# A trunk of two decoder layers: 28 of the 44 gate/value tile pairs of the up-projections as seven quarter products, with weights summed by accumulating DMAs

## The chip, the core and the metric

The kernel runs on one core of one Trainium2 chip. The metric is the device time of one execution in microseconds (us); lower is better. The core has a matrix engine (TensorE, PE in the rows, its weight loads PEld), three engines for elementwise work (VectorE: DVE, ScalarE: ACT, GpSimd: POOL), and a sync engine (SP) that issues most DMAs. Each engine works its instructions off in the order in which they were laid down when the program was built, and waits on semaphores for the others.

## The reference, cut to what matters

Two post-norm layers, each a mixer and then a gated feed-forward part with a short causal convolution. 512 tokens, model width 1024, inner width 2816, all in float32. The change touches the feed-forward part alone.

```python
def conv_ffn(x, w_up, conv_w, conv_b, w_down):
    h = causal_dwconv(x @ w_up, conv_w, conv_b)      # (512,1024) @ (1024,5632), width 3
    val, gate = jnp.split(h, 2, axis=-1)
    return (jax.nn.silu(gate) * val) @ w_down        # (512,2816) @ (2816,1024)
...
    for layer in range(DEPTH):
        y = even_mixer(...) if layer % 2 == 0 else odd_mixer(...)
        x = layer_norm(ALPHA * x + y, ln1_g[layer], ln1_b[layer])
        f = conv_ffn(x, ffn_w_up[layer], ffn_conv_w[layer], ffn_conv_b[layer], ffn_w_down[layer])
        x = layer_norm(ALPHA * x + f, ln2_g[layer], ln2_b[layer])
```

## The kernel before

Every float32 matrix product is made of three products of a shorter float32 type: each operand is split into a high part `hi` (a copy on ACT) and the rest `lo` (a subtraction, mostly on DVE), and hi·hi, lo·hi and hi·lo are summed in PSUM. `split` does this.

The activations lie transposed in four tiles, `xcur`: high part of model rows 0 to 511 and 512 to 1023, then the low parts, each 128 partitions x 4 blocks x 512 tokens. The up-projection of a layer has 44 weight tiles of 128 output channels, taken as 22 pairs (gate j, value j). For each tile, `mtile` calls `wload`, which has SP load 512 KB of weights into a `raw` tile (4 buffers) and splits it into `hi` and `lo` (5 buffers each); `mpass` then issues 24 matmuls of 128x128 weights against 512 columns into one PSUM bank. `conv` takes the bank through the convolution (one operation on ACT, two on DVE). Gate and value are multiplied on DVE, and the product is split once, ACT and POOL, into two of 44 `h` tiles that stay until the down part.

`proj_ln` is the down part with the norm behind it: for each of two halves of the model width it goes through 11 weight tiles of 256 inner rows. Each `wload` is followed by 24 matmuls against the `h` tiles. In the second layer's last tokens the 512 columns are taken as two pieces of 256 (`fine`, `parts`).

PSUM has eight banks under four names: `mm` (4 buffers), `S` (2), `tp` and `av`. The order on each engine is set by a scheduler when the program is built; tiles that are drawn from one pool under one tag take turns, and a tile that takes over memory waits until all readers of the tile before it are done. Tiles of a pool that has been closed give their memory to the next pool in the same way.

## Time and profile before

| | us |
|---|---|
| median of three runs | 1181.35 (1180.97 to 1182.17) |
| the profiled execution's own time | 1183.14 |
| its span in the profile | 1181.3 |
| PE busy / weight loads busy | 1156.3 / 941.3 |
| DVE / ACT / POOL busy | 691.6 / 466.7 / 193.7 |
| up part of layer 0 in one piece of the chain | 228.52, from 284.11 |

The profile's span leaves out 1.8 us of the execution's own time, and the profiled execution is itself 1.8 us above the median of the three runs. Busy matmul time overlaps itself, since a matmul's last columns drain while the next one starts; how fast matmuls follow each other is read from a piece of the chain and its count. "Idle before" in a group is time in which the engine waited before these instructions, with the releaser. In the chain, a step on PE that follows another on PE means that PE had work without a break.

### The profile page before, as it was taken

What the parts mean: (1) busy time and instruction counts of PE and PEld (TensorE: products, weight loads), DVE (VectorE), ACT (ScalarE), POOL (GpSimd) and SP (SyncE); (2) the same over time, 40 slices, a digit from 0 to 9 for tenths busy, and PEclk for the clock granted to TensorE, in tenths of its full rate; (3) what the DMA queues carried; (4) which work ended last, traced back from release to release, by engine and by line L of the source; (5) the groups of instructions that cost most, each with busy time, mean ns of one, the idle gap of its engine ahead of it and who ended that gap; (6) DMA issues with size and microseconds to landing.
All of it is one profiled execution on the core that took longest, in us unless ns stands there. A gap on an engine that the chain in (4) does not pass through costs nothing.

```text
span 1181.3 us, 13893 instructions
## 1 busy us (share of the span) xinstructions
PE 1156.3 (98%) x5312; PEld 941.3 (80%) x5312; DVE 691.6 (59%) x1098; ACT 466.7 (40%) x715; POOL 193.7 (16%) x234
## 2 busy tenths in 40 slices
PE   8999999999999999999998999999999999999997
PEld 6867778887888888888887866687888888888886
DVE  5987756477555555542338888768555455542326
ACT  5445653224444444431214466614444444432110
POOL 1122222211101110100003048112110111110002
PEclk9999999999999999999999999999999999999999
DMA  8331341213222232233222242213222322242201
GB/s 301 111 108 72 108 158 58 98 45 133 99 91 105 89 107 90 103 130 106 90 72 81 89 143 90 98 63 107 91 105 90 107 90 101 96 139 93 96 30 72
DMA packets 37570, 119.79 MB, mean 101 GB/s; under 512 B 4200, under 2 KB 4840, under 8 KB 37504
## 3 DMA queue, kind: packets, MB, share of 16 engines
q1 hardware_dynamic: 37344, 118.38, 28.9%
q8 instruction: 42, 0.69, 0.2%
q0 software_dynamic: 160, 0.52, 0.2%
q14 instruction: 24, 0.20, 0.1%
HBM read 116.75 MB, written 2.15 MB: 101 GB/s over the span
## 4 chain that ended last, share of the span: by engine, by line
PE 91%; DVE 6%; POOL 1%; issue 1%; ACT 1%; DMA 0%; POOLq 0%; SPq 0%; DVEq 0%; ACTq 0%
PE mm L238 53%; PE mm L330 14%; PE S L330 7%; PE tp L330 3%; PE av L330 2%; PE mm L278 1%; PE S L261 1%; PE mm L427 1%; PE av L852 1%; DVE lo L286 1%; PE av L550 1%; DVE xk L411 1%; PE S L634 1%; PE tp L650 1%; PE tp L536 1%
## 5 line engine op out<-in xcount | busy, mean ns | idle before, releaser
L238 PE MATMUL mm<-xT,hi 128*128 128x512 f32 (+1 forms) x1984 | 491.3, 395 | 0.5 <-ACT xT L285 0.5
L238 PEld LDWEIGHTS mm<-xT,hi 128*128 128x128 f32 x1984 | 371.0, 189 | 80.1 <-issue 4.4
L286 DVE TENSOR_TENSOR lo<-raw,hi 128x1024 fp32r<-128x1024 f32 (+1 forms) x201 | 234.5, 1171 | 174.5 <-ACT hi L285 174.3
L285 ACT ACTIVATE hi<-raw 128x1024 fp32r<-128x1024 f32 (+1 forms) x203 | 202.3, 999 | 205.4 <-PE mm L330 133.7
L981 DVE SCALAR_TENSOR_TENSOR tmp<-mm,col,tmp 128x510 f32<-128x510 f32 (+1 forms) x176 | 131.3, 749 | 207.9 <-ACT tmp L979 205.0
L238 PE MATMUL mm<-xT,lo 128*128 128x512 f32 (+1 forms) x992 | 249.4, 390 | 0.0
L238 PEld LDWEIGHTS mm<-xT,lo 128*128 128x128 f32 x992 | 185.0, 188 | 38.6 <-issue 1.9
L286 POOL TENSOR_TENSOR h<-tmp,h 128x512 fp32r<-128x512 f32 x44 | 57.7, 1311 | 433.4 <-ACT h L285 433.4
L979 ACT ACTIVATE tmp<-mm,col 128x512 f32<-128x512 f32 x88 | 68.4, 779 | 129.7 <-PE mm L238 128.4
L330 PE MATMUL mm<-hi,h 128*128 128x512 f32 (+1 forms) x396 | 118.0, 378 | 0.0
L330 PEld LDWEIGHTS mm<-hi,h 128*128 128x128 f32 x396 | 73.6, 188 | 13.7
L330 PE MATMUL mm<-lo,h 128*128 128x512 f32 (+1 forms) x198 | 74.8, 378 | 0.0
L314 POOL TENSOR_SCALAR small<-small 128x1 f32<-128x1 f32 (+2 forms) x25 | 14.5, 580 | 341.0 <-DVE small L404 279.5
L285 ACT ACTIVATE h<-tmp 128x512 fp32r<-128x512 f32 x44 | 27.8, 632 | 100.1 <-DVE tmp L990 100.1
L330 PE MATMUL S<-hi,h 128*128 128x512 f32 x176 | 56.9, 390 | 0.0
L330 PEld LDWEIGHTS mm<-lo,h 128*128 128x128 f32 x198 | 37.3, 188 | 6.8
L330 PE MATMUL mm<-hi,T 128*128 128x512 f32 x128 | 42.4, 399 | 0.0
L285 ACT ACTIVATE xT<-mm 128x512 fp32r<-128x512 f32 x24 | 13.5, 596 | 66.6 <-PE mm L427 66.4
L988 ACT ACTIVATE tmp<-tmp 128x512 f32<-128x512 f32 x44 | 27.9, 633 | 28.8 <-DVE tmp L981 28.8
L330 PEld LDWEIGHTS S<-hi,h 128*128 128x128 f32 x176 | 33.1, 188 | 6.7
L330 PE MATMUL S<-lo,h 128*128 128x512 f32 x88 | 34.3, 390 | 0.0
L411 DVE SCALAR_TENSOR_TENSOR xk<-xk,small,tmp 128x512 f32<-128x512 f32 (+1 forms) x33 | 29.0, 922 | 6.0 <-POOL small L315 6.0
(233 smaller groups left out, 1236.2 us busy)
## 6 DMA issues: line engine op xcount, KB each, us to landing
raw<-in_W SPq DMA_DIRECT2D x190, 512.0 KB, 3.5
bc<-dr SPq DMA_DIRECT2D x20, 256.0 KB, 3.9
tmp<-in_rows SPq DMA_DIRECT2D x16, 256.0 KB, 4.0
raw<-in_W SPq DMA_DIRECT2D x8, 256.0 KB, 5.7
xk<-in_x SPq DMA_DIRECT2D x4, 512.0 KB, 5.8
tmp<-in_xT SPq DMA_DIRECT2D x7, 256.0 KB, 6.3
out<-xk SPq DMA_DIRECT2D x7, 256.0 KB, 2.0
kc<-in_consts SPq DMA_DIRECT2D x1, 352.0 KB, 6.2
```

The costliest lines, as they stand in the source:

```text
L238: T.matmul(o[:, :cols_], w[:, k * P:(k + 1) * P], xs_(xcur, part, k)[:, :cols_], start=n == 0, stop=n == 3 * NK - 1)
L261: T.matmul(os[t], xs_(xcur, part, k)[:, t * P:(t + 1) * P], w[:, sl], start=k == 0 and n == 0, stop=k == NK - 1 and n == 2)
L278: T.matmul(os[t], xs_(xcur, part, k)[:, t * P:(t + 1) * P], w[:, kk * 512:(kk + 1) * 512], start=b == 0 and kk == 0 and n == 0, stop=b == ...
L285: A.activation(hi, src, AF.Copy)
L286: (lo_eng or V).tensor_tensor(lo, src, r32(hi), ALU.subtract)
L314: G.tensor_scalar(dst, var, EPS, None, ALU.add)
L330: T.matmul(o[:, c], a[:, t * P:(t + 1) * P], ww[:, kk * 512 + c.start:kk * 512 + c.stop], start=first and kk == 0 and n == 0, stop=fin and ...
L411: V.scalar_tensor_tensor(z[:, c], z[:, c], rs, shift[h][:, c], ALU.mult, ALU.add)
L427: T.transpose(tp[:, k * P:(k + 1) * P], z[:, k * P:(k + 1) * P], ident)
L979: A.activation(c, o, AF.Identity, bias=c1(cb + j), scale=c1(cw + 2 * 2 * NJ + j))
L981: V.scalar_tensor_tensor(c[:, d:], o[:, :S - d], c1(cw + (2 - d) * 2 * NJ + j), c[:, d:], ALU.mult, ALU.add)
L988: A.activation(gt, gt, AF.Silu)
```

## The change

Of the 22 pairs of a layer, pairs 0, 1, 4, 7, 10, 13, 16 and 19 stay as they are. The other 14 are taken two at a time, seven groups in a layer. In a group the tokens are cut in two halves of 256 (L, R) and the 1024 model rows in two halves, so that the activations are a block matrix A11, A12, A21, A22 (first number tokens, second rows), and the weights of one pair a block matrix of row half by gate or value. The product of two 2x2 block matrices is made from seven block products in place of eight (Strassen's way in Winograd's form): each is 12 matmuls of 256 columns for each of the two pairs, so 24 in a product and 168 in a group, where there were 96 of 512 columns. `mul` issues the 12.

Sums of activations (E, S2, S3, S4) are made once a layer, after pair 0: E and S2 on DVE, S3 and S4 in slices on POOL (`total`, `more`). S2 lies in a tile of tag `t`, and tag `t` has one buffer, which the weight tile `c` of each group takes over next. Sums of weights are made by DMAs that POOL issues and that add what they bring to what lies in the tile: three in a row on `c`, each after the split of what `c` held before, and one on `d`. The host only lays out the same weights in another order.

Partial results go from PSUM to `g` and `v` tiles by copies on ACT and sums on DVE, 256 columns each; the convolution then reads those. The gated products of a layer are kept unsplit in 11 tiles `act`. The down part splits them when it comes to them (ACT and POOL), once for each half of the model width, into 11 tiles of tag `s` in a pool that takes the memory of the up part's pool. In the listing below the changes of `proj_ln` are cut to `pieces`, which loads and splits the weights of one step and calls `two`.

```diff
+        def pieces(b, at):
+            hi, lo, _ = wload(at + b)
+            return hi, lo, two(b)
...
-        acts = []
-        for j in range(NJ):
-            gt = conv(NJ + j, 2 * j)
+        def gated(j, g, v):
+            gt = conv(NJ + j, g())
             A.activation(gt, gt, AF.Silu)
-            vl = conv(j, 2 * j + 1)
-            V.tensor_tensor(vl, vl, gt, ALU.mult)
-            hi = pool.tile([P, S], F32R, tag="h", name=nm("h"), bufs=2 * NJ)
-            lo = pool.tile([P, S], F32R, tag="h", name=nm("h"), bufs=2 * NJ)
-            split(vl, hi, lo, G)
-            acts.append((hi, lo))
-        proj_ln(acts, list(range(NJ)), dn, 2 * layer + 1, None if last else OD)
+            vl = conv(j, v())
+            V.tensor_tensor(act[j // 2][:, j % 2, :], vl, gt, ALU.mult)
+
+        with tc.tile_pool(name=f"up{layer}", bufs=1, side="left") as work:
+            up_quarters(work, up, gated)
+        after_ln[:] = [None, 0]
+        with tc.tile_pool(name=f"dn{layer}", bufs=1, side="left") as work:
+            def two(b):
+                hi, lo = (work.tile([P, 2, S], F32R, tag="s", name=nm("s"), bufs=11) for _ in range(2))
+                split(act[b], hi, lo, G)
+                return [(hi[:, i, :], lo[:, i, :]) for i in range(2)]
+            proj_ln(two, range(NJ), dn, 2 * layer + 1, None if last else OD)
+
+    def up_quarters(pool, up, gated):
...
+        gated(0, lambda: mtile(up), lambda: mtile(up + 1))
+        e, s2 = wide("e"), wide("t")
+        total(V, e, [(1, A22), (-1, A21)])
+        E, S2, S3 = pair(), pair(), pair()
+        split(e, *E)
+        more(V, s2, e, A11, ALU.add)
...
+        gated(1, lambda: mtile(up + 2), lambda: mtile(up + 3))
...
+        def mul(o, w, half, a, start=True):
+            n = 0
+            for ww, part in ((w[0], 0), (w[1], 0), (w[0], 1)):
+                for k in range(4):
+                    T.matmul(o[:, L], ww[:, half * 512 + k * P:half * 512 + (k + 1) * P], a[part][:, k, :],
+                             start=start and n == 0, stop=n == 11, skip_group_check=not start)
+                    n += 1
+
+        for j in range(3, NJ, 3):
+            js = (j - 1, j)
+            W11, W12, W21, W22 = (W[up + 2 * (j - 1) + i] for i in range(4))
+            if j == 3:
+                for i in range(4):
+                    sl = slice(i, i + 1)
+                    total(G, e[:, sl], [(1, [a[:, sl] for a in A11]), (-1, [a[:, sl] for a in A21])])
+                    split(e[:, sl], *(a[:, sl] for a in S3))
+                S4 = wide("e", F32R), wide("f", F32R)
+                for i in range(4):
+                    sl = slice(i, i + 1)
+                    more(G, s2[:, sl], s2[:, sl], [a[:, sl] for a in A12], ALU.subtract)
+                    split(s2[:, sl], *(a[:, sl] for a in S4))
+            c = pool.tile([P, D], F32, tag="t", name=nm("t"), bufs=1)
+            nc.sync.dma_start(c, W11)
+            e21, d, e22 = wraw(), wraw(), wraw()
...
+            nc.gpsimd.dma_start(d, W22, accum_op=ALU.add)
...
+            w = wsplit(c)
+            for i in range(2):
+                mul(x[i], w, i, A11)
+                A.activation(g[i][:, L], x[i][:, L], AF.Copy)
+            nc.gpsimd.dma_start(c, W12, accum_op=ALU.add)
+            w = wsplit(e21)
+            for i in range(2):
+                o = ps()
+                mul(o, w, i, A12)
+                V.tensor_tensor(g[i][:, L], g[i][:, L], o[:, L], ALU.add)
+            w = wsplit(c)
+            y = [ps() for _ in js]
+            for i in range(2):
+                mul(y[i], w, i, E)
+                A.activation(v[i][:, R], y[i][:, L], AF.Copy, scale=-1.0)
+            nc.gpsimd.dma_start(c, W22, accum_op=ALU.add)
+            w = wsplit(c)
+            for i in range(2):
+                mul(x[i], w, i, S2, False)
+                A.activation(v[i][:, L], x[i][:, L], AF.Copy)
+            nc.gpsimd.dma_start(c, W21, accum_op=ALU.add)
+            w = wsplit(c)
...
+            if j + 1 < NJ:
+                gated(j + 1, lambda: mtile(up + 2 * j + 2), lambda: mtile(up + 2 * j + 3))
```

In what follows P1 to P7 are the seven products of a group in the order of issue: P1 from `c` as loaded, P2 from `e21`, P3, P4 and P5 from `c` after its first, second and third accumulating DMA, P6 from `d`, P7 from `e22`.

Three places show how the order on the engines moves; all in layer 0.

First POOL, from the end of the norm into the up part. Before (`lo` is a weight tile's low part, `h` are the split products of pairs 0, 1 and 2):

```order
L315 TENSOR_TENSOR small_525_2527<-small_525_2527,phalf_81 128x1
L191 TENSOR_TENSOR lo_536_2590<-raw_534_2587,hi_535_2589 128x1024
L286 TENSOR_TENSOR h_541_2637<-tmp_539_2631,h_540_2636 128x512
L286 TENSOR_TENSOR h_553_2717<-tmp_551_2711,h_552_2716 128x512
L286 TENSOR_TENSOR h_565_2795<-tmp_563_2789,h_564_2794 128x512
```

And now (`e` becomes S3, `t_552` is S2 and becomes S4, `t_571` is the first group's `c`, `raw_573` its `d`; L1078, L1086, L1097 and L1102 are the accumulating DMAs):

```order
L191 TENSOR_TENSOR lo_547_2604<-raw_545_2601,hi_546_2603 128x1024
L1078 DMA raw_573_2784<-in_W 128x1024
L1027 TENSOR_TENSOR e_551_2650<-xT_508_2348 128x256 x2
L1029 TENSOR_TENSOR e_551_2650<-e_551_2650,xT_510_2350 128x256 x4
L1027 TENSOR_TENSOR e_551_2650<-xT_508_2348 128x256 x2
L1029 TENSOR_TENSOR e_551_2650<-e_551_2650,xT_510_2350 128x256 x4
L1032 TENSOR_TENSOR t_552_2651<-t_552_2651,xT_509_2349 128x256 x2
L1033 TENSOR_TENSOR t_552_2651<-t_552_2651,xT_511_2351 128x256 x2
L1032 TENSOR_TENSOR t_552_2651<-t_552_2651,xT_509_2349 128x256 x2
L1033 TENSOR_TENSOR t_552_2651<-t_552_2651,xT_511_2351 128x256 x2
L1086 DMA t_571_2781<-in_W 128x1024
L1097 DMA t_571_2781<-in_W 128x1024
```

The splits of the products are gone from here; 20 sums of 256 columns stand in their place, ahead of the first group's DMAs. SP's load of `t_571` waits for the last split of `t_552`.

Second DVE, between two groups, from the last plain pair's convolution on. Before, a pair goes by like this (`lo` are splits of weights, L981 the convolution, L990 the product):

```order
L981 SCALAR_TENSOR_TENSOR tmp_635_3245<-mm_634_3220,col_80,tmp_635_3245 128x511
L981 SCALAR_TENSOR_TENSOR tmp_635_3245<-mm_634_3220,col_80,tmp_635_3245 128x510
L286 TENSOR_TENSOR lo_664_3409<-raw_662_3406,hi_663_3408 128x1024
L990 TENSOR_TENSOR tmp_635_3245<-tmp_635_3245,tmp_630_3209 128x512
L981 SCALAR_TENSOR_TENSOR tmp_642_3285<-mm_641_3260,col_80,tmp_642_3285 128x511
```

Now, in the fourth group (`lo_720` is the split of `c` after its first accumulating DMA, with the convolutions L988 and the products L996 of the third group and of the plain pair behind it around it; `lo_724` is that after the second):

```order
L988 SCALAR_TENSOR_TENSOR tmp_691_3685<-g_664_3449,col_80,tmp_691_3685 128x510
L996 TENSOR_TENSOR a_538_2591<-tmp_690_3667,tmp_689_3662 128x512
L988 SCALAR_TENSOR_TENSOR tmp_692_3690<-v_666_3451,col_80,tmp_692_3690 128x511
L286 TENSOR_TENSOR lo_720_3846<-t_703_3767,hi_719_3845 128x1024
L988 SCALAR_TENSOR_TENSOR tmp_692_3690<-v_666_3451,col_80,tmp_692_3690 128x510
L988 SCALAR_TENSOR_TENSOR tmp_697_3726<-mm_696_3701,col_80,tmp_697_3726 128x511
L996 TENSOR_TENSOR a_538_2591<-tmp_692_3690,tmp_691_3685 128x512
L988 SCALAR_TENSOR_TENSOR tmp_697_3726<-mm_696_3701,col_80,tmp_697_3726 128x510
L286 TENSOR_TENSOR lo_724_3879<-t_703_3767,hi_723_3878 128x1024
L988 SCALAR_TENSOR_TENSOR tmp_702_3762<-mm_701_3737,col_80,tmp_702_3762 128x511
```

Each of these splits now has a DMA ahead of it and another behind it, and stands among the convolutions of the group before.

Third ACT, where the up part ends. Before, the last products (`h`) stand among the weight splits of the down part:

```order
L979 ACTIVATE tmp_791_4233<-mm_790_4208,col_80 128x512
L285 ACTIVATE hi_815_4372<-raw_814_4370 128x1024
L285 ACTIVATE h_792_4238<-tmp_791_4233 128x512
L285 ACTIVATE hi_818_4402<-raw_817_4400 128x1024
L285 ACTIVATE hi_821_4432<-raw_820_4430 128x1024
```

Now (L986 convolution, L994 silu of the last group's two pairs; `s_876` is the first split tile of the down part, which the first matmul there reads):

```order
L986 ACTIVATE tmp_868_5002<-v_842_4763,col_80 128x512
L994 ACTIVATE tmp_865_4974<-tmp_865_4974 128x512
L285 ACTIVATE hi_898_5157<-raw_897_5155 128x1024
L994 ACTIVATE tmp_867_4997<-tmp_867_4997 128x512
L285 ACTIVATE s_876_5021<-a_534_2587 128x1024
L285 ACTIVATE s_885_5059<-a_535_2588 128x1024
```

The split that the down part begins with now stands behind the last group's convolutions and silus. It takes memory of the up part's pool and waits for the last DVE read of `v_842`, the twelfth DVE instruction after P7's first half.

## Rows read from the trace of the kernel before

**Rows 1.** The page: busy time of engines, granted clock and DMA rate in 40 slices
```profile
PE 1156.3 (98%) x5312; PEld 941.3 (80%) x5312; DVE 691.6 (59%) x1098; ACT 466.7 (40%) x715; POOL 193.7 (16%) x234
...
PEclk9999999999999999999999999999999999999999
...
GB/s 301 111 108 72 108 158 58 98 45 133 99 91 105 89 107 90 103 130 106 90 72 81 89 143 90 98 63 107 91 105 90 107 90 101 96 139 93 96 30 72
```

**Rows 2.** The chain: shares by engine; pieces of layer 0 (start, length, what)
```profile
PE 91%; DVE 6%; POOL 1%; issue 1%; ACT 1%; DMA 0%; POOLq 0%; SPq 0%; DVEq 0%; ACTq 0%
...
284.11 228.52 PE mm L238 x1008
512.62 59.84 PE mm L330 x264
```

**Rows 3.** The chain in layer 1's last down part: matmuls of 256 columns
```profile
1116.75 0.71 PE av L330 x6
1117.47 0.72 PE mm L330 x6
```

**Rows 4.** Layer 0's up part: busy us (count) of PE, PEld, DVE, ACT, POOL; clock; DMA
```profile
284.11:512.62 228.51, 228.51 (x1009) 189.33 (x1009) 124.24 (x149) 100.82 (x128) 27.04 (x21) 1.00 0.28 99
```

**Rows 5.** Groups by shape in that stretch: busy us, mean ns, idle before
```profile
L238 PEld LDWEIGHTS mm<-xT,hi 128*128 128x128 f32 x671 | 126.0, 188 | 26.1
...
L286 DVE TENSOR_TENSOR lo<-raw,hi 128x1024 fp32r<-128x1024 f32 x42 | 51.4, 1223 | 2.0 <-ACT hi L285 2.0
L285 ACT ACTIVATE hi<-raw 128x1024 fp32r<-128x1024 f32 x41 | 43.2, 1053 | 0.0
L979 ACT ACTIVATE tmp<-mm,col 128x512 f32<-128x512 f32 x43 | 33.4, 779 | 62.5 <-PE mm L238 61.8 <-PE mm L211 0.7
L981 DVE SCALAR_TENSOR_TENSOR tmp<-mm,col,tmp 128x511 f32<-128x511 f32 x43 | 32.2, 750 | 99.5 <-ACT tmp L979 99.5
...
L990 DVE TENSOR_TENSOR tmp<-tmp,tmp 128x512 f32<-128x512 f32 x21 | 14.4, 686 | 1.4 <-ACT tmp L988 1.4
```

**Rows 6.** PE's timeline around the norm of layer 0
```profile
273.76 1.42 PE L427 MATMUL mm<-kc,xk 128*128 128x128 f32 x8 [2.03 <-issue]
275.07 3.58 PE L238 MATMUL mm<-xT,hi 128*128 128x512 f32 x8
278.49 2.01 PE L238 MATMUL mm<-xT,lo 128*128 128x512 f32 x8
```

**Rows 7.** DVE's timeline at the same place
```profile
264.46 1.42 DVE L411 SCALAR_TENSOR_TENSOR xk<-xk,small,tmp 128x512 f32<-128x512 f32 x2 [0.46 <-POOL small L315]
...
270.82 3.50 DVE L411 SCALAR_TENSOR_TENSOR xk<-xk,small,tmp 128x512 f32<-128x512 f32 x2 [0.46 <-POOL small L315]
...
276.65 1.88 DVE L286 TENSOR_TENSOR lo<-raw,hi 128x512 fp32r<-128x512 f32 x3
```

**Rows 8.** POOL: one timeline row there, and groups by shape of the whole span
```profile
270.76 2.35 POOL L191 TENSOR_TENSOR lo<-raw,hi 128x1024 fp32r<-128x1024 f32 x1
...
L834 POOL TENSOR_TENSOR tmp<-bc,kc 128x128 f32<-128x128 f32 x32 | 22.7, 744 | 47.7 <-DVE cv L736 47.6
...
L628 POOL TENSOR_TENSOR tmp<-bc,kc 128x128 f32<-128x128 f32 x16 | 6.8, 455 | 3.3 <-DMA bc<-dr 3.3
...
L919 POOL TENSOR_TENSOR pl<-pl 128x511 f32<-128x511 f32 x4 | 4.6, 1148 | 0.0
```

**Rows 9.** DMA issues: KB each, us from issue to landing
```profile
raw<-in_W SPq DMA_DIRECT2D x190, 512.0 KB, 3.5
...
tmp<-in_rows POOLq DMA_DIRECT2D x1, 256.0 KB, 4.7
pw<-in_poolw POOLq DMA_DIRECT2D x1, 256.0 KB, 3.1
```

**Rows 10.** DVE groups by shape of the whole span, sums from PSUM
```profile
L640 DVE TENSOR_TENSOR wt<-S,wt 128x512 f32<-128x512 f32 x4 | 2.8, 692 | 6.8 <-PE S L634 6.8
...
L640 DVE TENSOR_TENSOR wt<-S,wt 128x384 f32<-128x384 f32 x4 | 2.2, 558 | 0.0
```

More of the change, by code (lines that the diff above doesn't have):

```diff
@@ L320, in proj_ln @@
         nonlocal xcur
+        two = acts if callable(acts) else lambda b: [acts[k] for k in korder[2 * b:2 * b + 2]]
         npair = len(korder) // 2
@@ L353, in proj_ln @@
         for b in range(npair):
-            w = wload(blk + b)
             if needs:
+                w = wload(blk + b)
                 wv.need(*needs[b])
+                w = (*w[:2], two(b))
+            else:
+                w = pieces(b, blk)
             if b % half == 0:
@@ L391, in last @@
                     o = os[t]
-                mm(o, t, b, ws[i], b % half == 0, b % half == half - 1)
+                mm(o, t, ws[i], b % half == 0, b % half == half - 1)
                 if b % half == half - 1:
@@ L974, in ffn, with conv @@
         cw, cb = C_FW[layer], C_FB[layer]
-        def conv(j, m):
-            o = mtile(up + m)
+        act = [pool.tile([P, 2, S], F32, tag="a", name=nm("a"), bufs=NJ // 2) for _ in range(NJ // 2)]
+        def conv(j, o):
             c = tmp()
```

66 lines of the change are left out of this document (55 added, 11 removed).

## The prediction

> **What bounds the kernel now.** I read the page first: PE is busy 98% of the span at full clock throughout, DVE 59%, ACT 40%, DMA near 100 GB/s [rows 1]. The chain says which wait ends last: 91% of it is PE, and the whole up part of layer 0 is one piece, 1008 matmuls of 512 columns in 228.52 us, followed without a gap by the down part [rows 2]. So one such matmul takes 228.52/1008 = 0.2267 us and nothing else costs anything there; over the same stretch DVE is busy 124 and ACT 101 of 228.5 us [rows 4]. The up parts are PE-bound with no slack lost. A change gains only what it takes off PE, and loses every stall that it puts on it.
>
> **What comes off PE.** The only matmuls of 256 columns of this type stand in the last down part: 12 in 0.71 + 0.72 = 1.43 us, 0.119 each [rows 3]. A product is 24 of them, 2.86 us; a group 168, 20.0 us. Before, the same work was 96 x 0.2267 = 21.76 us. Each group gains 1.74 us, 14 groups **24.4 us**. That is less than the eighth in columns (2.7 us a group), since the part of a matmul's time that does not depend on columns is paid 1.75 times as often.
>
> **What comes onto DVE and ACT.** A group with the plain pair behind it has 9 weight splits where three pairs had 6, and 14 sums of 256 columns on DVE. By [rows 5] (split 1.22 us, convolution 0.75, product 0.69) and 0.42 for 256 columns (from 0.692 at 512 and 0.558 at 384, [rows 10]) DVE has 9 x 1.22 + 12 x 0.75 + 3 x 0.69 + some 10 x 0.42 = 26 us in a period of 20.0 + 10.9 = 30.9 us. It fits; what costs is the order, since each accumulating DMA waits for a DVE split and each split for the DMA before.
>
> **The time T of one accumulating DMA**, from POOL's issue to its landing, no row shows. Below it cannot be much under the plain 512 KB load, 3.5 us. Above I take twice the slower of the two POOL-issued loads, since those are of 256 KB: 9.4 us [rows 9]. In between: the faster POOL load, 3.1, plus another 256 KB at the first slice's 301 GB/s, 0.87, plus 512 KB of destination to be read as well, 1.74 [rows 1, 9]. T = **5.7**, nearest to those two POOL rows.
>
> A page gives a price of its own: the Trainium skill, "DMA: Bandwidth & Descriptors", section "Anatomy of one DMA — SWDGE (gpsimd) path", has 2.0 us plus bytes over 436 GB/s for a DMA that GpSimd issues, which is 3.2 us for 512 KB. By it, as an estimate, the sum below would come to 1211 us. The two POOL rows took 3.1 and 4.7 us where it gives 2.6, so I don't take it.
>
> **First group of a layer.** PE is free for P1 at 284.11 + 48 x 0.2267 = 295.0 us (tiles of pair 1). DVE can begin E when the norm's last split is done, at 276.65 [rows 7]: four sums and a split of 1024 columns at 1.22, two half weight splits at 0.63, so 284.0. Then POOL's 20 sums. Their shape is not in the trace; a sum of 128 columns takes 0.455 to 0.744, one of 511 takes 1.148 [rows 8]. I take 0.7 for 256: done at 298.0. (Bounds: 20 x 0.455 = 9 us, 20 x 1.148 = 23 us.) A slice split on ACT and DVE, 0.4 each: 298.8. Only now may SP load `c`: 3.5, then ACT's split 1.05 [rows 5]: P1 starts at 303.4, **8.4 us late**. From there the chain is split (DVE 1.22), T, split (ACT 1.05), three times, with nothing on PE to cover it but P1 to P4. P5 starts at 8.4 + 3 x (1.22 + T + 1.05) = 15.2 + 3T after PE was free, P7 ends 8.6 later; without waits it would be 20.0. Loss 3.8 + 3T = **20.9**.
>
> **Second group.** Count from the end of P5 of the first. PE returns to a P5 after P6, P7, the plain pair and P1 to P4: 5.7 + 10.9 + 11.4 = 28.0 us. The split of the new `c` stands on DVE behind P7's first sum: 4.3 + 0.42 + 0.75 + 1.22 = 6.7. The second split stands behind nine convolution steps, a sum, two products and a split, 9.8 us, so it ends at 17.7 whatever T is (up to 8.7). Then T, ACT and DVE split, T, ACT split: P5 can start at 21.0 + 2T. Loss 2T - 7.0 = **4.4**.
>
> **Third to seventh group.** Now `c` is split before P6's sums: the load starts when the third accumulation has been split (1.7 us before P5 ends) and lands at 1.8, splits end at 4.1. Then on DVE four sums, a split, two sums, six convolution steps, a product: 13.8, the second split 15.0. As before: 18.3 + 2T against 28.0. Loss 2T - 9.7 = 1.7 each, five groups **8.5**. The three waits end PE's idle time in P5; ACT and DVE stall behind the late split too, but what they hold up (the plain pair's PSUM) is wanted later than P5.
>
> **Start of the down part.** Before, PE ran on. Now the first matmul needs `s_876`, on ACT behind the last read of `v_842`. From the end of P7: a sum, six convolution steps, a product, a weight split 1.22, a last step, 7.6 us; ACT's split 1.05; and the third matmul needs POOL's low part, 2.35 [rows 8]. Less two matmuls: **10.5 us**. Later splits run five tiles ahead (2.35 on POOL against 5.4 on PE), so they, and doing them twice, cost nothing; were that cover gone, each of 22 would cost up to 2.35.
>
> **The clock.** After 2.03 us without matmuls and eight small transposes PE's next eight matmuls took 3.42 us, 0.427 each, 1.2 GHz, and the ones after that 2.4 GHz again: 1.6 us lost [rows 6]. Most stalls above are of that length. Inside a group the lost time hides under the next wait; it counts after P5 of the first and second group and at the down part: 3 x 1.6 = **4.8**.
>
> **Sum.** A layer loses 20.9 + 4.4 + 8.5 + 10.5 + 4.8 = 49.1 us, two layers 98.2, less 24.4: +73.8. The profiled execution took 1183.1, so 1256.9; it stood 1.8 above the median: **1255 us**. At T = 3.5 the losses are 14.3, 0, 0, 10.5 and 2 x 1.6: 1213. At T = 9.4 they are 32.0, 11.8, 45.5, 10.5 and 4.8: 1366. Above T = 5 a microsecond of T costs 30.
>
> **The rivals.** (a) The accumulations are as quick as plain loads and only the starts cost: 1213. For it: the DMA engines are three quarters idle [rows 4]. Against: POOL's own loads.
>
> (b) The accumulations are slow, T of 7.5 and more, and the chain sets the period of every group: 1309 to 1366. Two DMAs, that on `d` and that on `c`, can be in flight together.
>
> (c) POOL's sums are held up by DVE. Beside POOL's 2.35 us operation two DVE operations took 3.50 where they take 1.42 elsewhere [rows 7, 8], and a POOL sum of 128 columns ranges from 0.455 to 0.744. Here DVE has about 6.4 us of work on two SBUF operands during the sums; if POOL stands still for it, each layer starts that much later: 1268. The Trainium skill states the rule in "SBUF — State Buffer", section "Who interferes with whom": a DVE instruction with two SBUF inputs contends with a GpSimd one that reads SBUF, and the second to issue waits. The trace agrees by these rows.
>
> (d) Weight loads bind at 256 columns. One takes 188 ns [rows 5], longer than 119. Then a group is 168 x 0.188 = 31.6 us, 9.8 more than before, 137.5 in all. Products of 4.5 us cover more: a first group loses 15.2 + 3T - 18.0 = 14.3, later ones nothing, the down part 10.5, the clock 3.2; 1375. Against: 12 in a row at 0.119.
>
> (e) Faster: both long waits are for memory that a later tile takes over, `c` from S2 and `s_876` from `v`. If neither binds, a layer loses 3T - 4.6, and 2T - 7 where that is positive; at T = 3.5 the time is 1169. It decides below T = 4.8. Against: the order shows both tiles behind the readers.
>
> **How the numbers follow.** Likeliest, T between 4.5 and 7: 0.57 (own range 1225 to 1295). (a) 0.15, (b) 0.10, (c) 0.08, (d) 0.02, (e) 0.06, nothing that can be told 0.02. A measurement of this kernel tells about 0.2% from no change. Faster 0.06, same 0.02, slower 0.92. The range is 1200 to 1320: it takes in (a), (c) and the lower edge of (b), and leaves out most of (b), (d), (e) and the unchanged time, 0.18.
>
> **What would show it.** L1055 matmuls at about 0.119 each; POOLq rows L1086, L1097, L1102 landing after 5 to 6 us; two PE waits of 8 to 10 us in each layer, one ended by ACT's split of the first `c`, one by the first `s` tile; in each group a short wait in P5. Wrong would be: T far from 5.7, POOL's sums far from 14 us in all, or matmuls of 256 columns that don't keep 0.119 over a product.

## The result, and the profile after

The changed kernel takes **1316.75 us** (median; 1314.63 to 1322.02) beside 1181.36 before: a ratio of 1.115, 95% interval 1.112 to 1.119. The forecast was 1255 with a range of 1200 to 1320, slower with a chance of 0.92. So the direction held and the time lies at the range's upper end, 62 us above the number. The profiled execution took 1314.97 us with a span of 1313.2, 131.9 more than the span before.

The page of the kernel after, its engines, the granted clock in 40 slices and the chain by engine, as in [rows 1, 2]:

```profile
PE 1182.9 (90%) x6320; PEld 1009.4 (77%) x6320; DVE 835.2 (64%) x1282; ACT 563.1 (43%) x889; POOL 327.9 (25%) x330
PEclk9999999997989898979999999997789899989999
DMA 11%; PE 11%; DVE 3%; issue 2%; ACT 2%; POOL 1%; POOLq 0%; DVEq 0%; ACTq 0%
```

PE is no longer busy without a break. The chain of this page could be followed back to 931.58 us only, so its shares sum to 30% of the span; in that stretch, most of layer 1's up part and what follows, the DMAs, most of them those that fill `t`, the tile of `c`, take as much as PE, which had 91% of the whole before. The clock, full in the up parts before, is below full in slices of both up parts. The view of waits of the kernel after (engine, operand and line that waited, on whom: sum, times, longest) shows where PE stood:

```profile
PE S L1055 <- ACT hi L285: 31.3, 5, 12.5
PE mm L1055 <- DVE tmp L988: 29.0, 10, 4.5
PE mm L334 <- ACT s L285: 20.3, 2, 10.2
PE tp L1055 <- ACT hi L285: 15.0, 5, 4.1
PE mm L1055 <- ACT hi L285: 3.3, 2, 1.8
PE mm L334 <- POOL s L286: 2.4, 2, 1.2
```

With three smaller ones (1.0, 0.9 and 0.5) these are 103.7 us, and none of them is there before. The first row is mostly the late P1 of each layer, the third the start of each down part, the fourth P5. The second, ten waits of 2.9 us in P3, was not forecast.

Behind these waits PE worked at half clock for a time. The windows of layer 0's up part in which the granted clock was 0.50 (length, then busy time of PE, PEld, DVE, ACT and POOL, granted clock, DMA), five of ten, with the sum over all ten, and the sum over the eleven of layer 1:

```profile
298.83:312.48 13.65, 5.18 (x23) 5.06 (x24) 5.86 (x8) 3.88 (x6) 3.53 (x5) 0.50 0.28 58
370.51:377.34 6.83, 5.32 (x23) 5.02 (x24) 5.37 (x5) 5.78 (x8) 0.00 (x0) 0.50 0.37 121
438.78:445.60 6.82, 6.09 (x28) 6.12 (x29) 3.02 (x5) 2.18 (x3) 0.30 (x1) 0.50 0.45 79
548.00:551.42 3.42, 3.42 (x16) 3.42 (x17) 1.23 (x3) 0.00 (x0) 0.00 (x0) 0.50 0.94 157
565.07:578.72 13.65, 4.36 (x10) 2.99 (x11) 7.54 (x12) 9.64 (x12) 5.57 (x3) 0.50 0.47 155
sum 64.85, PE 43.00 PEld 40.82 DVE 29.92 ACT 27.25 POOL 11.42; mean PE 4.30 PEld 4.08 DVE 2.99 ACT 2.72 POOL 1.14
...
sum 71.68, PE 47.38 PEld 45.44 DVE 31.97 ACT 26.95 POOL 14.47; mean PE 4.31 PEld 4.13 DVE 2.91 ACT 2.45 POOL 1.32
```

PE worked 43.0 + 47.4 = 90.4 us at half clock, so 45.2 us went there; the rest of those windows is time in which PE stood anyway. Waits 103.7 plus clock 45.2 less the forecast gain of 24.4 is 124.5 of the 131.9. Of the rest, 2.4 is that a group gains 1.57 us and not 1.74 (see the experiment with plain tiles); 5.0 stay open. This sum tells where PE's time went. It does not tell what caused it: the time of most groups is set by a chain that PE has no part in, as the rest of this section shows, and there half clock only takes the place of waiting.

How a group now runs is seen where each P7 begins. From the timeline of PE, the first four matmuls of P7 in the first, second and seventh group of layer 0:

```profile
340.36 0.64 PE L1055 MATMUL mm<-e,hi 128*128 128x256 f32 x4
...
380.40 0.64 PE L1055 MATMUL mm<-e,hi 128*128 128x256 f32 x4
...
559.91 0.64 PE L1055 MATMUL mm<-e,hi 128*128 128x256 f32 x4
```

From the second to the seventh is 179.5 us, 35.9 a group, where PE's own work is 31.07. Why is seen in one period. The accumulations of the fourth group on POOL (start, length of the issue, what POOL waited for before):

```profile
417.36 0.87 POOL L1078 DMA_DIRECT2D raw<-in_W  x1 [15.03 <-DMA raw<-in_W]
417.90 1.24 POOL L1086 DMA_DIRECT2D t<-in_W  x1
430.14 0.87 POOL L1097 DMA_DIRECT2D t<-in_W  x1 [11.00 <-DVE lo L286]
438.21 0.87 POOL L1102 DMA_DIRECT2D t<-in_W  x1 [7.20 <-DVE lo L286]
```

L1086, the first accumulation on `c`, could have gone when the split of `c` was done, at 415.54. It stands behind the one on `d` (L1078), which waits for `d`'s load, and is then in flight together with it. From issue to landing, over 14 groups, for L1086 and then L1097:

```profile
L1086 POOL DMA_DIRECT2D t<-in_W x14: 847/1194/1241, 309.0 to 1132.9; - x14
DMA to landing us min/median/max: 5.4/9.1/10.6
...
L1097 POOL DMA_DIRECT2D t<-in_W x14: 846/860/873, 318.7 to 1145.6; - x14
DMA to landing us min/median/max: 5.2/5.3/5.5
```

An accumulation that is alone takes 5.3 us, counted from the start of its issue (forecast 5.7). L1086 takes 9.1 in the median; in the ten groups where `d`'s was sent 0.54 us before it, 8.8 to 10.6. SP's loads run beside it there too. The timeline of all engines shows what follows, here from the second split of `c` in the fourth group to P3's second half:

```profile
427.52 1.06 ACT L285 ACTIVATE hi<-t 128x1024 fp32r<-128x1024 f32 x1 [6.41 <-DMA t<-in_W]
...
428.62 1.23 DVE L286 TENSOR_TENSOR lo<-t,hi 128x1024 fp32r<-128x1024 f32 x1 [4.72 <-ACT hi L285]
...
435.60 1.06 ACT L285 ACTIVATE hi<-t 128x1024 fp32r<-128x1024 f32 x1 [2.46 <-DMA t<-in_W]
...
436.69 1.23 DVE L286 TENSOR_TENSOR lo<-t,hi 128x1024 fp32r<-128x1024 f32 x1 [4.27 <-ACT hi L285]
...
437.83 1.53 DVE L988 SCALAR_TENSOR_TENSOR tmp<-mm,col,tmp 128x511 f32<-128x511 f32 x2
...
439.51 0.55 PE L1055 MATMUL mm<-o,hi 128*128 128x256 f32 x1 [3.78 <-DVE tmp L988]
```

DVE waits 4.27 us for the third split, and behind it stand the last convolution steps of the plain pair. They hold a PSUM bank of the ring `mm`, and P3's second half takes it next: PE waits 3.78 us there, not in P5. From the end of one P5 split of `c` on DVE (409.15) to the end of the next (445.74) is 36.6 us: the chain of load, splits and accumulations is longer than PE's 31.07. In the third to seventh group of layer 0 it is 36.3 us in the mean, and PE has no step in it: SP's loads start as the P5 split ends, `d`'s is the third of them, POOL sends L1078 some 0.6 us after that has landed and L1086 0.5 us later; behind each accumulation on `c` ACT's split, DVE's split and the next accumulation follow within 0.1, 0.1 and 0.3 us.

### The profile page after: what moved, and what is told of

It reads as the page before. It is cut to its first block, busy times and chain, and to the rows that moved or that the text cites. A ratio compares the mean times of both kernels' runs of the same rounds, so it can differ in the third digit from the quotient of the medians.

```text
span 1313.2 us, 16580 instructions
## 1 busy us (share of the span) xinstructions
PE 1182.9 (90%) x6320; PEld 1009.4 (77%) x6320; DVE 835.2 (64%) x1282; ACT 563.1 (43%) x889; POOL 327.9 (25%) x330
## 5 line engine op out<-in xcount | busy, mean ns | idle before, releaser
L238 PE MATMUL mm<-xT,hi 128*128 128x512 f32 (+1 forms) x1088 | 281.7, 400 | 0.5 <-ACT xT L285 0.5
L238 PEld LDWEIGHTS mm<-xT,hi 128*128 128x128 f32 x1088 | 201.9, 191 | 44.6 <-issue 4.4
L286 POOL TENSOR_TENSOR s<-a,s 128x1024 fp32r<-128x1024 f32 x44 | 107.2, 2446 | 142.0 <-PE mm L334 72.9
L334 PE MATMUL mm<-hi,s 128*128 128x512 f32 (+1 forms) x396 | 121.6, 387 | 22.7 <-ACT s L285 20.3
L238 PE MATMUL mm<-xT,lo 128*128 128x512 f32 (+1 forms) x544 | 138.8, 391 | 0.0
L238 PEld LDWEIGHTS mm<-xT,lo 128*128 128x128 f32 x544 | 101.0, 188 | 21.4 <-issue 1.9
L334 PEld LDWEIGHTS mm<-hi,s 128*128 128x128 f32 x396 | 75.4, 194 | 38.5 <-issue 20.6
L1055 PE MATMUL S<-o,hi 128*128 128x256 f32 x448 | 76.3, 308 | 6.6 <-ACT hi L285 6.6
L334 PE MATMUL mm<-lo,s 128*128 128x512 f32 (+1 forms) x198 | 76.4, 386 | 0.0
L1055 PEld LDWEIGHTS S<-o,hi 128*128 128x128 f32 x448 | 68.9, 219 | 7.3 <-ACT hi L285 7.3
L1078 POOL DMA_DIRECT2D raw<-in_W x14 | 12.3, 876 | 192.6 <-DMA raw<-in_W 74.3
L1055 PE MATMUL S<-xT,hi 128*128 128x256 f32 x224 | 36.6, 300 | 24.6 <-ACT hi L285 24.6
L988 DVE SCALAR_TENSOR_TENSOR tmp<-mm,col,tmp 128x511 f32<-128x511 f32 (+1 forms) x64 | 47.2, 745 | 7.9 <-ACT tmp L986 7.4
```

Source lines behind the costliest of these rows:

```text
L238: T.matmul(o[:, :cols_], w[:, k * P:(k + 1) * P], xs_(xcur, part, k)[:, :cols_], start=n == 0, stop=n == 3 * NK - 1)
L286: (lo_eng or V).tensor_tensor(lo, src, r32(hi), ALU.subtract)
L334: T.matmul(o[:, c], a[:, t * P:(t + 1) * P], ww[:, kk * 512 + c.start:kk * 512 + c.stop], start=first and kk == 0 and n == 0, stop=fin and ...
L988: V.scalar_tensor_tensor(c[:, d:], o[:, :S - d], c1(cw + (2 - d) * 2 * NJ + j), c[:, d:], ALU.mult, ALU.add)
L1055: T.matmul(o[:, L], ww[:, half * 512 + k * P:half * 512 + (k + 1) * P], a[part][:, k, :], start=start and n == 0, stop=n == 11, skip_group ...
L1078: nc.gpsimd.dma_start(d, W22, accum_op=ALU.add)
```

## The experiments

| run | us, median | ratio to before, 95% |
|---|---|---|
| after | 1316.75 | 1.1152 (1.1115 to 1.1188) |
| d_second | 1285.51 | 1.0861 (1.0827 to 1.0895) |
| p2_banks | 1320.06 | 1.117 (1.115 to 1.1191) |
| no_add (sums left out) | 1236.35 | 1.0463 (1.0439 to 1.0488) |
| plain_tiles (sums left out) | 1204.78 | 1.0196 (1.0158 to 1.0234) |
| ring8 | 1319.62 | 1.1169 (1.1149 to 1.1189) |
| down_wp | 1297.99 | 1.0971 (1.0912 to 1.1029) |
| late_sums | 1268.75 | 1.0727 (1.0709 to 1.0745) |
| pool_sums | 1228.23 | 1.0388 (1.0371 to 1.0404) |
| pool_all | 1220.57 | 1.0321 (1.0294 to 1.0348) |
| pool_front | 1212.74 | 1.027 (1.0256 to 1.0284) |
| pool_front_s2 | 1198.68 | 1.015 (1.0133 to 1.0167) |
| six_groups | 1179.41 | 0.9982 (0.9973 to 0.9991) |

### What sets the period of a group

**d_second.**

```diff
-            nc.gpsimd.dma_start(d, W22, accum_op=ALU.add)
...
-            nc.gpsimd.dma_start(c, W12, accum_op=ALU.add)
+            first = nc.gpsimd.dma_start(c, W12, accum_op=ALU.add).ins
+            with tc.issue_after(first):
+                nc.gpsimd.dma_start(d, W22, accum_op=ALU.add)
```

> Only change: in each group POOL sends the accumulation on d behind the first accumulation on c, not ahead of it. Theory A (the chain on the one tile c sets the period of each group, and its first accumulation takes 9.1 us and starts 2.3 us late because d's is ahead of it in POOL's queue; the other two take 5.3): first accumulation on c falls to 5.3 to 6, the period of groups 3 to 7 from 36.5 to about 31.5 us, the waits in the second half of P3 (13 us in a layer) go, a wait of 0 to 2 us in P5 may stay, half clock goes with them; 1250 to 1265 us. Rival B (the waits in P3 come from DVE's order alone: the plain pair's last convolution step stands behind the split for P4, and holds the PSUM bank): less than 10 us changes, 1305 to 1317. Rival C (the accumulations load the DMA engines so that any order costs the same): 1317, and another of the four accumulations takes 9 us in a wait that counts.

31 us came back, not 52 to 67 (the time lies in no expected range). Landing times in d_second of the first accumulation on `c` and of `d`'s behind it:

```profile
L1085 POOL DMA_DIRECT2D t<-in_W x14: 857/872/957, 309.4 to 1108.7; - x14
DMA to landing us min/median/max: 5.3/6.9/7.7
...
L1087 POOL DMA_DIRECT2D raw<-in_W x14: 850/1139/1200, 310.1 to 1109.3; - x14
DMA to landing us min/median/max: 7.4/9.6/11.2
```

So the one behind still takes over 9 us, and the one ahead 6.9 in place of 5.3. But it is not the accumulation behind it that costs the one ahead. In the second group of either layer the trace has no packet of SP's loads while the one ahead was in flight. It took 5.5 and 5.4 us there, and the one behind it 7.4 and 7.5. In the first group of the kernel after, L1086 had no other accumulation beside it but a load that SP sent 0.62 us later, and took 7.0. One of each, in layer 0:

```profile
L1085 POOL DMA_DIRECT2D t<-in_W x1: 867/867/867, 346.0 to 346.0; - x1
DMA to landing us min/median/max: 5.5/5.5/5.5
```
```profile
L1086 POOL DMA_DIRECT2D t<-in_W x1: 887/887/887, 309.0 to 309.0; - x1
DMA to landing us min/median/max: 7.0/7.0/7.0
```

So an accumulation lost some 2 us to one sent 0.6 us ahead of it, and 0 to 2.4 to SP's loads beside it; L1086 has both in most groups. In the twelve other groups of d_second SP's loads ran beside the one ahead, and it took 5.3 to 7.7; what tells these apart no run shows.

The period fell to 32.8 us in layer 0 and 33.4 in layer 1, and the waits in P3 from 29.0 us to 3.2, while those of P5 on ACT rose from 15.0 to 20.7. That is theory A with a smaller share. Rival B is out: P3's waits went though DVE's order had not been touched.

**p2_banks.**

```diff
             for i in range(2):
-                o = ps()
+                o = ps(("tp", "av")[i])
                 mul(o, w, i, A12)
```

> The kernel after with P2's two results in the PSUM banks tp and av, so that P3's second half takes a bank of the ring mm that is free two tiles earlier and no longer waits for the plain pair's last convolution step. Rival B (DVE's order and the bank are the cause): the 13 us of waits in P3 go and nothing takes their place, the period falls from 36 to 32.5, 1265 to 1285 us. Theory A (the chain on c sets the period): the wait moves to P4 and P5, the period stays at 35.5 to 36.5, 1308 to 1320 us.

PE's waits from the second to the seventh group in layer 0, first p2_banks, then the kernel after:

```profile
PE tp L1055 <- ACT hi L285: 19.7, 6, 4.2
PE S L1055 <- ACT hi L285: 1.1, 1, 1.1
```
```profile
PE mm L1055 <- DVE tmp L988: 13.1, 5, 3.8
PE tp L1055 <- ACT hi L285: 4.5, 2, 3.9
```

The waits on the bank are gone, PE waits in P5 instead, and the kernel is no faster, as theory A had it. The bank was only where the chain's lateness met PE.

**no_add.** The four lines keep everything but `accum_op`.

```diff
-            nc.gpsimd.dma_start(c, W12, accum_op=ALU.add)
+            nc.gpsimd.dma_start(c, W12)
```

> Leaves the sums of weights out, in another way: the same four DMAs from POOL in the same places, but they overwrite the tile in place of adding to it. It prices the adding. If the adding costs the reading of the destination: 3.2 to 4 us in place of 5.3, the first on c 6 to 7 in place of 9.1, the period falls by 5 to 6 us to PE's own 31, and the time to 1230 to 1255. If the adding costs nothing and 5.3 is POOL's own way of sending a DMA: 5.3 stays, 1310 to 1320.

Without the adding the accumulation at L1097 takes 3.7 us:

```profile
L1097 POOL DMA_DIRECT2D t<-in_W x14: 527/527/530, 316.0 to 1068.1; - x14
DMA to landing us min/median/max: 3.6/3.7/4.7
```

So adding costs 1.6 us of 5.3 (the forecast had put 1.74 for reading 512 KB of destination), and 0.33 of POOL's time for the issue, 0.86 in place of 0.53. From the third group on the period is 31.1, and the time lies in the lower of the two expected ranges. The Trainium skill's price for a DMA that GpSimd issues ("DMA: Bandwidth & Descriptors", "Anatomy of one DMA — SWDGE (gpsimd) path"), 3.2 us as an estimate for this size, is near the 3.7 of the plain DMA and far from the 5.3 of the adding one; the measurement decides.

**plain_tiles.**

```diff
-            nc.gpsimd.dma_start(c, W12, accum_op=ALU.add)
...
-            w = wsplit(c)
+            w = wsplit(tile(W12))
```

(`tile` loads its argument into a new `raw` tile; the same in the six other places.)

> Leaves the sums of weights out: each of the seven products takes its weights from a raw tile of its own, by plain loads that SP issues; no accumulation, no tile c. Same matmuls, same splits, as many loads. Theory A: without the chain only the start of the down part still waits (10.2 us a layer) and perhaps P6 or P7 of the first group for their sums on POOL; the first P1 no longer waits for memory; 1183 - 24 + 2 x 10.2 + 2 x (2 to 5) = 1183 to 1195 us, matmuls of 256 columns at 0.12. Rival B (DVE's order and PSUM): waits in the second half of P3 stay at 2 to 4 us a group, 1215 to 1240. Rival D (the seven products themselves are slower than priced, by weight loads or DVE): no waits to speak of and still above 1200.

Four periods of layer 0 without the chain, from the third P7 to the seventh, as a window:

```profile
384.30:508.50 124.20, 124.20 (x866) 116.63 (x865) 93.38 (x129) 72.02 (x104) 0.00 (x0) 1.00 0.50 153
```

No wait, full clock, P7 to P7 31.07 us. Three pairs took 3 x 48 x 0.2267 = 32.64 before, so a group gains **1.57 us**. Rival D falls, and weight loads (116.6 of 124.2) do not bind. The time came out 10 us above the expected range: the first group still lost some 10 us a layer, 5.0 of it waits in P3 and P4, nearly all on DVE's splits and a convolution step, the rest half clock.

### The start of the down part

**ring8, then down_wp.**

```diff
-                hi, lo = (work.tile([P, 2, S], F32R, tag="s", name=nm("s"), bufs=11) for _ in range(2))
+                hi, lo = (work.tile([P, 2, S], F32R, tag="s", name=nm("s"), bufs=8) for _ in range(2))
```
```diff
+            early = [True] * 2
             def two(b):
-                hi, lo = (work.tile([P, 2, S], F32R, tag="s", name=nm("s"), bufs=11) for _ in range(2))
+                if early:
+                    early.pop()
+                    hi, lo = (wp.tile([P, 2, S], F32R, tag=t, name=nm("s"), bufs=5) for t in ("hi", "lo"))
+                else:
+                    hi, lo = (work.tile([P, 2, S], F32R, tag="s", name=nm("s"), bufs=11) for _ in range(2))
```

> Only change: 8 in place of 11 tiles of tag s in the down part, so that none of them lies on the memory of v and g. Theory (the wait of 10.2 us at the start of each down part is for v's memory): the wait goes, or falls to under 2 us, with the half clock around it (2.2 us); 2 x (10.2 + 2.2) = 25 us less, 1290 to 1297. Rival (the first splits stand late in ACT's order anyway, behind the last pair's work): the wait stays above 6 us, 1305 to 1317. Rival (8 tiles are too few and the down part waits within): waits of PE on s tiles later in the down part, over 1317.

> The only change to the kernel after: the first two pairs of activations of a down part are split into tiles of the weights' ring (tags hi and lo), the rest into the 11 tiles of tag s as before. Theory (the wait of 10.2 us at the start of the down part is for the opening of the new pool as a whole, which takes in the last read of v, not for the bytes that a tile takes over; 8 tiles clear of v left it unchanged): now nothing of the first two pairs waits for the pool, PE has 10.9 us of work while the third pair's split waits for it; the wait falls from 10.2 and 1.2 to under 2 us together and the half clock behind it goes: 2 x (9.5 + 2.2) = 23 us less, 1290 to 1297 us. Rival (ACT has no room for the early splits, they delay the last group's): the wait moves into P5 to P7 of the last group, 1305 to 1320.

ring8 gained nothing. Its 8 tiles take 32 of the 44 KB a partition that the up part's pool had; laid out in the order of the program, these are the bytes of `e`, `t` and `o`, and none lies on `g` or `v`. Still the first split follows the last read of `v` (DVE's last convolution step ends at 573.49, ACT's split starts at 573.58). In waits of PE, ring8 over its whole span and then down_wp from 500 to 700 us:

```profile
PE mm L334 <- ACT s L285: 20.9, 2, 10.9
```
```profile
PE mm L334 <- POOL s L286: 2.1, 1, 2.1
```

So, by these two runs, a new pool opens when the old one as a whole has been read for the last time. down_wp, which takes two pairs out of that pool, removes the wait but for 2.1 us at the third pair, and 19 us of the time, a little under the expected 20 to 27.

### The first group of a layer

**late_sums** (d_second, and:)

```diff
-                    more(G, s2[:, sl], s2[:, sl], [a[:, sl] for a in A12], ALU.subtract)
-                    split(s2[:, sl], *(a[:, sl] for a in S4))
+                        q = pool.tile([P, 256], F32, tag="q", name=nm("q"), bufs=1)
+                        G.tensor_tensor(q, r32(S2[0][:, i]), r32(S2[1][:, i]), ALU.add)
+                        more(G, q, q, [a[:, i] for a in A12], ALU.add)
+                        A.activation(S4[0][:, i], q, AF.Copy, scale=-1.0)
+                        V.scalar_tensor_tensor(S4[1][:, i], q, -1.0, r32(S4[0][:, i]), ALU.mult, ALU.subtract)
```

with the whole block moved behind the first accumulation on `c`.

> The kernel d_second (d's accumulation behind the first on c) with the start of the first group changed: S4 is made on POOL from the split S2 in a tile of its own, so that tile t is free for c from the start, and POOL makes S3 and S4 behind the first accumulation (24 sums in place of 20). Theory (the first group loses 28 us a layer because c waits for POOL's sums and the chain then runs with nothing to cover it): P1 starts without a wait, the chain starts some 15 us sooner, P5 of the first group waits 5 to 10 us; 2 x (14 to 18) less than d_second's 1285: 1250 to 1258 us. Rival (POOL's sums, in its one queue, now hold up the second and third accumulation): waits in P4 and P5 of 8 us and more, 1265 to 1285.

17 us less than d_second: about half of what was expected, and a time in the rival's range. P1's wait fell from 12.2 us in the kernel after to 1.8, so the memory of `t` had held it up. But the first accumulation went at 297.86, 11.6 us sooner than in d_second and not 15, since on DVE the split of `c` (296.09) stood behind convolution steps of pair 1 that were not ready sooner; P3, P4 and P5 then waited 5.5, 3.5 and 3.4 us. Moving the load exposed the queue behind it.

### Sums of weights on POOL in place of DMAs

**pool_sums.**

```diff
-            nc.gpsimd.dma_start(c, W12, accum_op=ALU.add)
+            G.tensor_tensor(c, c, d, ALU.add)
+            G.tensor_tensor(d, d, e22, ALU.add)
...
-            nc.gpsimd.dma_start(c, W22, accum_op=ALU.add)
+            G.tensor_tensor(c, c, e22, ALU.add)
...
-            nc.gpsimd.dma_start(c, W21, accum_op=ALU.add)
+            G.tensor_tensor(c, c, e21, ALU.add)
```

> The kernel after with the four accumulating DMAs of a group replaced by four sums of 128x1024 on POOL from the raw tiles that are loaded anyway (no load more, four DMAs fewer, result the same). Theory A (the length of a link of the chain, issue 0.9 + 5.3 us, sets the period of a group): a link becomes a sum of about 2.4 us, the chain ends before PE needs it from the second group on, the period falls from 36 to 31.1 us; the late P1 (12 us) and the down part's start (10 us) stay; 1183 - 24 + 2 x (17 to 22 first group + 13 down) = 1219 to 1232 us. Rival (POOL's sums and DVE's operations on two SBUF operands hold each other up, as two DVE operations took 3.50 beside a POOL operation where 1.42 was usual): DVE's 24 us a period become 31 and more, waits on DVE's splits and convolution steps stay in every group, 1250 to 1300.

As theory A had it. Two of POOL's groups over five periods of layer 0 (busy, mean ns, idle before), and the window of the same five:

```profile
L1086 POOL TENSOR_TENSOR raw<-raw,raw 128x1024 f32<-128x1024 f32 x5 | 15.5, 3106 | 1.2 <-DMA raw<-in_W 0.9
L1102 POOL TENSOR_TENSOR t<-t,raw 128x1024 f32<-128x1024 f32 x5 | 12.0, 2408 | 12.2 <-DVE lo L286 12.2
```
```profile
363.50:518.80 155.30, 155.30 (x1082) 145.83 (x1081) 138.33 (x161) 87.62 (x130) 53.85 (x20) 1.00 0.32 101
```

Two of the three links on `c` are 2.4 us in place of 5.3 (not 6.2, as the expectation has it: the 5.3 include the issue), the other 2.8, and PE runs 155.3 us without a wait. The contention is real: DVE is busy 27.7 us a period where plain_tiles has 23.3 in 31.05, beside 10.8 us of POOL, and `d`'s sum takes 3.1 us. That agrees with the rule of the Trainium skill ("SBUF — State Buffer", "Who interferes with whom"), but 27.7 still fits in 31.1, so it costs no time here.

**pool_all** is pool_sums with the block of late_sums and with down_wp; **pool_front** adds pair 19 ahead of the first group; **pool_front_s2** is pool_front with the sums of activations as in the kernel after; **six_groups** is pool_front_s2 with pairs 20 and 21 plain and taken first (the second diff; the loop's bound is changed in the host's layout too).

```diff
         gated(1, lambda: mtile(up + 2), lambda: mtile(up + 3))
+        gated(NJ - 3, lambda: mtile(up + 2 * NJ - 6), lambda: mtile(up + 2 * NJ - 5))
...
-            if j + 1 < NJ:
+            if j + 1 < NJ - 3:
```
```diff
-        gated(1, lambda: mtile(up + 2), lambda: mtile(up + 3))
+        for j in 1, NJ - 2, NJ - 1:
+            gated(j, lambda: mtile(up + 2 * j), lambda: mtile(up + 2 * j + 1))
...
-        for j in range(3, NJ, 3):
+        for j in range(3, NJ - 1, 3):
```

> pool_sums with both other mends: S4 from the split S2 with POOL's sums behind the first sum on c, and the first two pairs of the down part split into tiles of the weights' ring. Theory: only the first group still loses something (POOL makes 24 sums of activations and 4 of weights there, 24 to 28 us in its one queue): 5 to 10 us a layer with its half clock, and the down parts 0 to 2; 1183 - 24 + 2 x (5 to 12) = 1169 to 1183 us, so from 1% faster than the kernel before to the same. Rival (DVE and POOL hold each other up): 1195 to 1250, with waits on DVE in every group.

> pool_all with the order of the pairs changed: the plain pair 19 is taken before the first group in place of between the sixth and the seventh, so that 10.9 us more of PE's work lie ahead of the first group (the sixth and the seventh then follow each other without a plain pair between). Theory (in pool_all the first group still loses 20 us a layer, nearly all of it a wait in P4 for a sum on c that stands behind some 14 sums of activations on POOL, so that 10.9 us of cover take most of it): first group 4 to 8 us in place of 20, the others 31.1 us as they are, the seventh 20.2 us where the chain of sums (about 20 us) keeps up and 2 to 4 us more where it does not; 1183 - 22 + 2 x (5 to 11) = 1171 to 1183 us, 0 to 1% faster than the kernel before. Rival (POOL's queue is the bound there, so the cover only lets it start later; or the seventh group without a plain pair loses what the first gains): 1195 to 1215.

> pool_sums with the first two pairs of the down part in the weights' ring and plain pair 19 before the first group, S4 from S2 in tile t as in the kernel after, so c's first load still waits for POOL's sums. In pool_sums that ended with P1 at 308.0, 13 us after PE was free at 295; with the plain pair PE is free at about 306, so 2 us remain, and 3 to 5 us in P3 to P5 behind it, with half clock 1 to 3; 1183 - 22 + 2 x (6 to 11) = 1173 to 1183 us. Rival as for pool_front: 1195 to 1215. If the order on POOL (c's sums behind the activations' here, among them there) is what matters, this one is 5 to 10 us a layer better than pool_front.

> pool_front_s2 with six groups in place of seven: pairs 20 and 21 become plain pairs and are taken, like pair 1, ahead of the first group, and pair 19 is the last of the up part again (the host's layout leaves 20 and 21 as they were). So PE is free for P1 at about 317, when POOL's sums (301) and the first split of c (308 to 311) are done, no two groups follow each other without a plain pair, and the up part's pool is read for the last time while the last plain pair runs. Theory (what was lost in pool_front_s2 is the late start, 10.6 us a layer, the seventh group without a plain pair before it, 4.3, and the start of the down part, 2.2; the seven products themselves gain 1.57 us a group at a period of 31.07 us): 6 x 1.57 = 9.4 us a layer won, 1 to 5 us lost in the first two groups and the down part's start; 1182 - 18.8 + 2 x (1 to 5) = 1165 to 1173 us, 0.7 to 1.4% faster than the kernel before. Rival (the first group loses its 5 to 10 us whatever lies ahead of it, because its four splits and sums on c queue behind the plain pairs' work on ACT and DVE): 1174 to 1185.

pool_all missed by 38 us: only 8 better than pool_sums, of which the down part alone should have given 20. PE's long wait in its first group, and the sum on POOL that P4 waited for:

```profile
319.05 2.08 PE L1061 MATMUL S<-o,hi 128*128 128x256 f32 x8 [11.88 <-ACT hi L285]
```
```profile
298.28 2.71 POOL L1081 TENSOR_TENSOR t<-t,raw 128x1024 f32<-128x1024 f32 x1 [25.32 <-DVE lo L286]
...
315.39 2.52 POOL L1106 TENSOR_TENSOR t<-t,raw 128x1024 f32<-128x1024 f32 x1
```

Between the two stand 14 sums of activations and `d`'s. In pool_front the cover of 10.9 us did not help: the same sum went at 316.50, and the wait was P3's second half, 12.4 us. The convolution that holds its bank stood on ACT behind the split of that sum (ACT's step at 320.00, DVE's last until 324.72, P3's second half at 324.87), so the order on the engines, not the start, was the bound. In pool_front_s2, where the activations' sums come first and `c`'s after them, the same cover takes the first group from 20 to 10.6 us; the seventh group without a plain pair costs 24.6 us in place of 20.2. It is 7.0 us a layer better than pool_front, as the last sentence of its expectation has it, but both missed their forecast of 1171 to 1183 and 1173 to 1183, and lie in the rival's range. six_groups runs every group in 31.07 us; what is left in its first is one wait in P3, 3.26 us, with half clock behind it:

```profile
PE mm L1062 <- DVE tmp L988: 6.5, 2, 3.3
PE mm L334 <- DVE tmp L988: 3.3, 2, 1.7
```

At 1179.41 us it is the one version under the kernel before, by 0.18% (0.09 to 0.27): about what a measurement can tell. That is less than expected, and a time in the rival's range. Twelve groups gain 18.8 us; waits of 6.5 + 3.3 + 1.8 in both layers, and 2.9 + 1.7 of half clock behind them, give 16.2 of it back.

## Why the prediction was right, and where its size was off

The mechanism was the forecast one: seven products take less of PE, and the stalls around the accumulations cost several times that. That the time lies in the stated range is in part luck. At the measured T of 5.3 the working gives some 1243 us, 74 too few; the range of 1200 to 1320 took in the lower edge of rival (b), and that is where the time lies. One layer by the prediction's terms, from the P7 starts above, with 312.3 for a first P7 without stalls (295.0 and six products of 2.88):

| layer 0, us | forecast | measured |
|---|---|---|
| seven groups' matmuls | -12.2 | -11.0 |
| first group | 20.9 | 28.1 |
| second group | 4.4 | 9.0 |
| third to seventh | 8.5 | 24.2 |
| start of the down part | 10.5 | 10.4, and 3.4 behind it (1.2 of wait, 2.2 of half clock) |
| clock | 4.8 | in the rows above |
| sum | 36.9 | 64.1 |

The other 67.8 us of the span's 131.9 are layer 1's and the little outside. In the measured column a row has its half clock in it. Of the 27.2 us that this layer missed, the third to seventh group have 15.7.

- **The gain.** 256 columns follow each other at 0.12 us, as the row of 12 had it; 22.0 us in all for 24.4. Rival (d) is out.
- **T.** 5.3 us for one accumulation alone, 5.7 forecast; the split of that sum into a POOL load and 1.74 for the destination came out as 3.7 and 1.6. Rival (a) is out.
- **First group.** POOL's sums began at 284.10 (284.0 forecast) and took 17.4 us, not 14; P1 began at 307.30, forecast 303.4. Beside DVE's convolution steps four sums took 2.82 us; beside DVE's sum of two SBUF operands at 287.74 two took 2.87, and that operation of DVE took 1.66 where those before it took 1.21 to 1.23. So the hold-up of rival (c) was there, at about half its price, though no run took DVE's work away. From P1 to P7 it then took 33.1 us where the working has 29.6: the first accumulation took 7.0 beside a load of SP, each accumulation went 0.3 to 0.6 us behind its split, and PE ran at half clock from 332.96 to 336.38, behind the wait in P5.
- **Third to seventh group: the step that failed.** It took T for each of three accumulations, and let the second split of `c` end 15.0 us after P5 whatever T was. But the first accumulation is sent behind `d`'s, with SP's loads beside both, and takes 9.1; and it starts 0.9 to 3.1 us after its split, because POOL waits for `d`'s load. In the fourth group that second split ended 18.1 us after P5 (429.85, from 411.70). Rival (b) had noted that two DMAs can be in flight together; the sum had no price for it. So the chain set the period of every group after all, as rival (b) said, and the time lies in (b)'s range of 1309 to 1366, but with T at 5.3: a period of 35.9 us, forecast 32.6. d_second, which only swaps the two, gives back 31 us; no_add and pool_sums, with shorter links, bring the period to 31.1.
- **The place of the wait.** Forecast in P5; it was in P3's second half, by a PSUM bank behind DVE's late split. p2_banks shows that the place did not matter. The prediction had said that what a late split holds up is wanted later than P5; that was wrong.
- **The down part.** 10.2 us of wait for 10.5. But the reason was read too narrowly: not `v`'s bytes, the whole pool (ring8).
- **The clock.** Forecast 9.6 in two layers; PE lost 45.2 of its own time, in ten or eleven stretches a layer, where the forecast had three losses of 1.6 us, from one stretch of 3.42 us [rows 6]. Yet this is not a loss on top of the rows above. 19 of the 45 us lie in the third to seventh groups and 11 in P1 to P4 of the first, all ahead of a wait for a chain that has no step on PE; slower work there only shortened that wait, as the forecast had said of the inside of a group. At most the other 15 us could lengthen the time. They lie behind P5 of the first and second group and at the start of the down part, where the forecast had put its 9.6.
- **Rival (e)** is out: both long waits were there.

## What to carry to other kernels

Price a serial chain of DMAs by what else is in flight: the same accumulation took 5.3 us alone, 7.0 beside a plain load, 7.4 behind another accumulation and some 9 with both. A chain that is just longer than PE's work in a period costs PE in every period, wherever the wait surfaces; the remedy is a shorter link (here a sum on an idle engine, 2.4 us) more than another place for the wait. Where such a chain sets the pace, do not add PE's half clock to its loss. And a saving of 1.57 us a group pays only if its start-up is covered by work that is there anyway.

## What the runs showed of the hardware that was not expected

- An accumulating DMA of 512 KB from POOL takes 1.6 us longer than the plain one (5.3 and 3.7) and its issue holds POOL for 0.86 us in place of 0.53. With no load of SP beside them, two sent 0.6 us apart took 5.4 to 5.5 and 7.4 to 7.5 (d_second); one alone beside a load of SP took 7.0 (kernel after, both first groups); one sent 0.54 us behind another, with loads of SP beside it, 8.8 to 10.6.
- After stalls of 3.8 to 3.9 us in layer 0 the granted clock was 0.50 for 6.8 us, after 2.0 and 2.4 us for 3.4; a period whose waits were 1.22, 0.66 and 0.51 us showed none. After the waits of 10 to 12 us it was 13.65, partly within the wait. In sum PE lost 45 us to half clock beside 104 of waits, but 30 of the 45 lie ahead of a wait for the chain and lengthened nothing.
- POOL's 10.8 us of sums a period made DVE's same work 4.4 us longer.
